# Low-rank products and head sums of a recurrence layer over all 128 columns of TensorE, in a four-layer model kernel

## The chip, the cores and the metric

The kernel runs on one core of one Trainium2 chip. The metric is the device time of one execution in microseconds (us). Before the change the median of 3 runs is 2441.49 us (2440.22 to 2445.58).

## The reference

The reference is a forward pass of four layers over 512 tokens of width 1024, in float32. Each layer has a mixer and a gated feed-forward net. The four mixers differ: a recurrence (RWKV-7), attention with a sliding window, a gated unit over chunks, and gated linear attention. The change touches the recurrence alone, `rwkv7_mix`, which computes, cut to what matters:

```python
xx = token_shift(x) - x
xr, xw, xk, xv, xa, xg = (x + xx * mu[c] for c in range(6))
r, k, v = jnp.einsum('cbsd,cde->cbse', jnp.stack([xr, xk, xv]), w_rkv).astype(f32)
w = -jax.nn.softplus(-(w0 + jnp.tanh(xw @ w1) @ w2).astype(f32)) - 0.5
a = jax.nn.sigmoid((a0 + (xa @ a1) @ a2).astype(f32))
g = jax.nn.sigmoid(xg @ g1) @ g2
kk = hs(k * k_k)
kk = kk * lax.rsqrt(jnp.maximum(jnp.sum(kk * kk, -1, keepdims=True), 1e-24))
```

There are 16 heads of 64 channels. `w1` and `a1` are 1024 x 64 and `g1` is 1024 x 128: these are the low-rank products. The sum of `kk * kk` over the channels of a head is the head sum. After this a state of 64 x 64 per head is carried over the 512 tokens; the kernel does that in chunks of 64 tokens, with a small triangular inverse for each.

## The kernel before

**Arithmetic.** Each float32 operand is split into a high and a low part of TensorE's faster float32 kind (`F32R`): ScalarE (ACT) copies the high part, VectorE (DVE) subtracts it to get the low one (`split`, line 617). A product is then three matmuls, high by high, high by low and low by high (`mm3`, line 621). `weights` (line 603) loads a weight of up to 1024 columns by a DMA on SyncE's queue (SP) and splits it. The recurrence stage has three raw buffers (`wraw`) and two buffers each for the high and low parts (`whi`, `wlo`), line 1066; 24 buffers of 512 columns (`slot`) hold split operands and, later, the work tiles of the recurrence (line 1067 and 1156).

**The recurrence stage**, `rwkv` (line 1050), in the order in which it is written:

1. `token_squares`, `rstd`: the norm of x. Constants: `sel`, 30 columns of zeros with two columns of ones for the two heads of a 128-row tile, and `selr`, its copy as F32R (lines 1075 to 1079).
2. For each of the eight 128-row tiles of x (line 1099): the normed tile `hn[k]`, its shifted difference `xx[k]`, the split of the weight rows `rw_w_k`, the mixed operand (`mixed`, line 1083: one DVE instruction for x + xx * mu, then a split), and 24 matmuls into the eight PSUM banks of the key product K.
3. Head sums (line 1113): for each of the eight tiles of K, ACT squares it, it is split, and two matmuls with 16 columns of `selr` as weights add into 16 rows of one bank.
4. The receptance product R in eight blocks `n` (line 1121), each with its own weight (`gemm`, line 627, 24 matmuls) over the same eight mixed operands. Between the blocks stand the tail of the head sums (line 1123: a copy of 16 rows, four transposes of 16 rows, the inverse root on DVE) and the low-rank products `lora` (line 1090): the one of `w1` behind block 0, of `a1` behind block 2, of `g1` behind block 4. Each loads and splits its weight and mixes its own eight operands, for 24 matmuls. The two 64-column products write 64 rows of a bank; their results are the two halves of `twa`.
5. The mixed operands of the value product V (line 1138).
6. `ahead(0)` (line 1158): for the first four heads `rwkv_prepare` (decays, from `twa` and the head sums), `rwkv_products`, `rwkv_inverse` (a long series of small DVE instructions) and `rwkv_direct`. Then the V product in two halves (line 1182), which is dense work for TensorE (PE).
7. Four times: `ahead(n + 1)`, and beside it `rwkv_chain` of n (line 1388), which walks the chunks in turn; at each, ACT copies PSUM results into `wu`, `tok` and `vu`, which the next matmuls need. `rwkv_out` (line 1459) finishes a group; its ACT instructions write `out`.
8. The output product, and then the feed-forward net and the other layers.

**Order.** The written order is not the order of issue. `Program` records all instructions and plans them (`run`, line 320): at each step it takes, over all engines, the instruction that could start first by its table of costs. On one engine the candidates are sorted by their turn, which is the number of the instruction as recorded plus the offset that the table `TURNS` (line 32) gives for its range of numbers; a candidate with a later turn is taken only where it could start over 200 ns sooner (`SLACK`). So a large positive offset makes a block filler, and a negative one puts it ahead. Buffers bound it too: an instruction isn't planned before a buffer of its pool is free. Where PE would idle, `keep_warm` and `ahead_of_cold` (lines 435 and 459) put in idle matmuls of `ident` (line 533).

By the recorded numbers the blocks of the change stand so: 0 to 408 are steps 1 to 3 with the mixing for R; 409 to 436 block 0 of R; 437 to 488 the low-rank product of `w1`; 489 to 516 block 1; 517 to 532 the tail of the head sums; 533 to 560 block 2; 561 to 612 `a1`; 613 to 640 block 3; 641 to 668 block 4; 669 to 720 `g1`; 721 to 804 blocks 5, 6 and 7; 805 to 852 the mixing for V; 853 to 910 `rwkv_prepare` of `ahead(0)`; 1236 to 1359 and 1360 to 1483 the halves of V. Later, 1499 to 1556, 2161 to 2218 and 2823 to 2880 are the three other `rwkv_prepare`, and 2090 to 2157, 2752 to 2819 hold the `rwkv_out` of groups 0 and 1's walks.

## Time and profile before

| | us |
|---|---|
| median of 3 runs | 2441.49 |
| the profiled execution | 2440.58 |
| its span, first to last instruction | 2438.9 |
| around the span | 1.7 |
| PE busy in the span | 2393.9 (98%) |
| DVE busy | 1952.3 (80%) |
| ACT busy | 1458.3 (60%) |
| granted TensorE clock, mean | 0.999 of full |

The recurrence stage takes about the first 436 us of the span. All instructions carry the line of the recording helper (L263), so groups are told apart by the names of their tiles: `ps<-slot,whi` is a matmul into a PSUM bank with the moving operand in a `slot` and the weights in `whi`. The form `128*64 128x512` is a matmul with 128 rows and 64 columns of weights, over 512 moving columns. `rw_w` is the tensor `rw_w1` or `rw_w2`, `rw_a` is `rw_a1` or `rw_a2` (the profile drops the number). Busy times of PE are modelled and overlap; where the pace of matmuls matters, the starts and their counts are used.

### The profile page before, as it was taken

What the parts mean: (1) busy time and instruction counts of PE and PEld (TensorE: products, weight loads), DVE (VectorE), ACT (ScalarE), POOL (GpSimd) and SP (SyncE); (2) the same over time, 40 slices, a digit from 0 to 9 for tenths busy, and PEclk for the clock granted to TensorE, in tenths of its full rate; (3) what the DMA queues carried; (4) which work ended last, traced back from release to release, by engine and by line L of the source; (5) the groups of instructions that cost most, each with busy time, mean ns of one, the idle gap of its engine ahead of it and who ended that gap; (6) DMA issues with size and microseconds to landing.
All of it is one profiled execution on the core that took longest, in us unless ns stands there. A gap on an engine that the chain in (4) does not pass through costs nothing.

```text
span 2438.9 us, 37676 instructions
## 1 busy us (share of the span) xinstructions
PE 2393.9 (98%) x14250; PEld 1974.5 (81%) x14250; DVE 1952.3 (80%) x3052; ACT 1458.3 (60%) x2389; POOL 337.7 (14%) x395
## 2 busy tenths in 40 slices
PE   9999999999999999999999999999999999999997
PEld 8677789988887759878777788898888888988885
DVE  8787875786889889768689879987868979886868
ACT  4656765665556697645466435755546756665554
POOL 0000000221212002112111300211111111221110
PEclk9999999999999999999999999999999999999999
DMA  5210013789986159889877836888997776998993
GB/s 174 77 61 10 6 39 109 151 219 233 207 223 168 36 142 201 208 202 218 199 181 190 219 101 148 182 218 212 221 227 192 176 178 141 207 211 218 223 220 87
DMA packets 128759, 404.55 MB, mean 166 GB/s; under 512 B 14512, under 2 KB 21680, under 8 KB 128576
## 3 DMA queue, kind: packets, MB, share of 16 engines
q0 software_dynamic: 51840, 176.18, 40.5%
q1 hardware_dynamic: 76736, 225.95, 27.4%
q8 instruction: 112, 1.84, 0.3%
q14 instruction: 71, 0.58, 0.1%
HBM read 397.62 MB, written 2.10 MB: 164 GB/s over the span
## 4 chain that ended last, share of the span: by engine, by line
PE 82%; DVE 7%; ACT 5%; issue 3%; DMA 2%; SPq 0%; POOL 0%; POOLq 0%; DVEq 0%; ACTq 0%
PE ps L263 82%; DVE slot L263 2%; DVE wlo L263 2%; ACT slot L263 1%; DMA wraw<-ffn_w_a 1%; DVE h L263 1%; ACT et L263 1%; ACT whi L263 1%; ACT out L263 1%; DVE left L263 1%; DMA wraw<-ffn_o_b 1%; ACT vu L263 0%; DVE et L263 0%; SPq L263 0%; DMA slot<-x 0%
## 5 line engine op out<-in xcount | busy, mean ns | idle before, releaser
L263 PE MATMUL ps<-whi,slot 128*128 128x512 f32 (+1 forms) x4944 | 1505.6, 385 | 11.8 <-ACT whi L263 6.4
L263 PEld LDWEIGHTS ps<-whi,slot 128*128 128x128 f32 x4944 | 916.6, 188 | 186.7 <-ACT whi L263 11.5
L263 ACT CAST whi<-wraw 128x1024 fp32r<-128x1024 f32 (+3 forms) x686 | 678.5, 997 | 573.5 <-PE ps L263 494.1
L263 DVE TENSOR_TENSOR wlo<-wraw,whi 128x1024 fp32r<-128x1024 f32 (+3 forms) x686 | 787.7, 1159 | 223.8 <-ACT whi L263 214.0
L263 PE MATMUL ps<-wlo,slot 128*128 128x512 f32 (+1 forms) x2472 | 929.1, 384 | 3.0 <-DVE wlo L263 2.8
L263 PEld LDWEIGHTS ps<-wlo,slot 128*128 128x128 f32 x2472 | 464.1, 188 | 88.3 <-DVE wlo L263 10.5
L263 PE MATMUL ps<-slot,whi 128*128 128x512 f32 (+3 forms) x976 | 280.6, 367 | 1.8 <-ACT slot L263 1.0
L263 PEld LDWEIGHTS ps<-slot,whi 128*128 128x128 f32 (+2 forms) x976 | 171.7, 184 | 40.0 <-DVE slot L263 3.0
L263 DVE TENSOR_TENSOR h<-h,ps 128x512 f32<-128x512 f32 x256 | 169.1, 682 | 29.9 <-PE ps L263 27.7
L263 DVE TENSOR_TENSOR slot<-ps,slot 128x512 f32<-128x512 f32 (+1 forms) x237 | 151.1, 650 | 44.2 <-PE ps L263 36.7
L263 POOL DMA_DIRECT2D wraw<-ffn_w_a x128 | 110.5, 873 | 514.1 <-DVE wlo L263 351.9
L263 PE MATMUL ps<-slot,wlo 128*128 128x512 f32 (+3 forms) x488 | 176.0, 365 | 0.1
L263 DVE TENSOR_TENSOR slot<-left,slot 128x512 fp32r<-128x512 f32 x254 | 160.1, 655 | 15.8 <-ACT slot L263 13.6
L263 ACT CAST slot<-left 128x512 fp32r<-128x512 f32 (+1 forms) x254 | 145.5, 600 | 33.1 <-DVE left L263 20.3
L263 ACT COPY slot<-ps 128x512 f32<-128x512 f32 (+3 forms) x168 | 89.1, 545 | 70.1 <-PE ps L263 69.0
L263 POOL DMA_DIRECT2D wraw<-ffn_w_b x64 | 55.0, 871 | 477.2 <-DMA wraw<-ffn_w_b 353.4
L263 PEld LDWEIGHTS ps<-slot,wlo 128*128 128x128 f32 (+2 forms) x488 | 89.6, 184 | 16.6 <-DVE wlo L263 1.7
L263 PE MATMUL ps<-ident,slot 128*128 128x128 f32 (+1 forms) x672 | 99.4, 267 | 3.1 <-DVE slot L263 2.9
L263 DVE TENSOR_TENSOR slot<-slot 128x512 fp32r<-128x512 f32 (+5 forms) x152 | 89.7, 613 | 7.0 <-ACT slot L263 5.0
L263 POOL DMA_DIRECT2D wraw<-ffn_o_a x64 | 55.6, 869 | 283.0 <-DVE wlo L263 180.4
L263 PEld LDWEIGHTS ps<-ident,slot 128*128 128x128 f32 (+1 forms) x672 | 67.4, 139 | 31.2 <-DVE slot L263 14.0
L263 DVE SCALAR_TENSOR_TENSOR slot<-slot,ncol 128x512 f32<-128x512 f32 (+1 forms) x96 | 66.9, 705 | 20.9 <-ACT slot L263 19.7
(285 smaller groups left out, 2190.6 us busy)
## 6 DMA issues: line engine op xcount, KB each, us to landing
wraw<-ffn_w_a SPq DMA_DIRECT2D x128, 512.0 KB, 6.0
wraw<-ffn_w_a POOLq DMA_DIRECT2D x128, 512.0 KB, 8.1
wraw<-ffn_o_a SPq DMA_DIRECT2D x64, 512.0 KB, 5.6
wraw<-ffn_o_a POOLq DMA_DIRECT2D x64, 512.0 KB, 6.6
wraw<-ffn_w_b SPq DMA_DIRECT2D x64, 384.0 KB, 4.7
wraw<-ffn_w_b POOLq DMA_DIRECT2D x64, 384.0 KB, 7.0
wraw<-ffn_o_b SPq DMA_DIRECT2D x16, 512.0 KB, 4.7
wraw<-ffn_o_b POOLq DMA_DIRECT2D x16, 512.0 KB, 7.9
```

The source lines that it names most:

```text
L263: op = self.add(eng.name, lambda: getattr(eng.target, what)(*map(real, args), **{k: real(a) for k, a in kw.items()}), *self.price(eng.name ...
```

## The change

- The head sums use 128 columns of weights and write all 128 rows of a bank. `selr` is now a `slot` of 142 columns: the 30 of `sel`, and zeros behind them that a second DVE copy writes. The tail copies 128 rows, makes four full transposes and reads the 16 wanted columns of each block.
- `w1` and `a1` go side by side into one raw tile by two DMAs (runs of 64 elements), are split together, and each of the two low-rank products uses all 128 columns, of which one half is used afterwards. Both are now written behind block 0 of R; `g1` is behind block 3 instead of 4.
- In the loop over the tiles of x, the mixed operand is written ahead of the split of the weight rows.
- With this the program has one instruction more ahead of number 410 and one fewer in all, so the ranges of `TURNS` shift, and the offsets of the recurrence stage are others. Those beyond number 4250 are the old ones, shifted by one.

In the numbering after the change, 410 to 437 is block 0 of R, 438 to 441 the loading of `w1` and `a1`, 442 to 490 the product of `w1`, 491 to 539 that of `a1`, 540 to 567 block 1, 568 to 583 the tail of the head sums, 584 to 611 block 2, 612 to 639 block 3, 640 to 691 `g1`, 692 to 719 block 4, 720 to 803 blocks 5 to 7; from 804 on each number is one less than before.

```diff
-    (0, 97, -207), (97, 193, -192), (193, 289, -140), (289, 409, -148), (437, 489, 1044), (489, 517, 10155), (517, 533, 2661), (533, 561, -359),
-    (561, 613, 1728), (641, 669, 1548), (669, 721, -310), (749, 777, 10951), (805, 853, 3322), (853, 911, 7335), (1190, 1236, -146),
-    (1236, 1360, -3686), (1360, 1484, 1692), (1499, 1557, 1650), (1557, 1577, -519), (1883, 1988, -731), (1988, 2090, -249), (2090, 2158, 1863),
-    (2161, 2219, 5511), (2239, 2259, -947), (2378, 2498, -3564), (2498, 2545, 2492), (2650, 2752, 2436), (2752, 2820, 5854), (2823, 2881, 3201),
-    (2881, 2901, -434), (2901, 2921, -32), (2921, 3040, 124), (3040, 3160, 418), (3207, 3312, -307), (3312, 3414, 300), (3414, 3483, 250),
-    (3483, 3588, -390), (3729, 3769, 843), (3886, 3999, 812), (4131, 4190, 149), (4350, 4449, 12), (4449, 4548, 141), (4548, 4647, -229),
...
+    (0, 98, -14563), (98, 194, -6331), (194, 290, -5109), (290, 410, -2326), (494, 540, 573), (568, 584, 3450), (612, 640, 6446), (640, 720, -1503),
+    (720, 748, 4169), (748, 776, -1620), (804, 852, 517), (852, 910, 9960), (910, 930, -70), (1189, 1235, -292), (1235, 1359, -995),
+    (1359, 1483, 955), (1498, 1556, 913), (1556, 1576, -521), (1835, 1882, 1053), (1882, 1987, -932), (1987, 2089, 433), (2089, 2157, 909),
+    (2160, 2218, 4894), (2377, 2497, -1662), (2497, 2544, 1319), (2544, 2649, -600), (2649, 2751, 2954), (2751, 2819, 9075), (2822, 2880, 7892),
+    (2920, 3039, 870), (3311, 3413, 750), (3413, 3482, 1012), (3627, 3728, 1237), (3728, 3768, 1131), (3772, 3885, -1758), (3998, 4112, 1412),
+    (4189, 4248, 51), (4349, 4448, 12), (4448, 4547, 141), (4547, 4646, -229), (4646, 4745, -100), (4745, 4844, -86), (4844, 4943, -93),
...
@@ -1075,8 +1074,9 @@
         nc.vector.memset(sel, 0.0)
         nc.vector.memset(sel[:64, 14:15], 1.0)
         nc.vector.memset(sel[64:, 15:16], 1.0)
-        selr = one("selr", F32R, 30)
-        nc.vector.tensor_copy(selr, sel)
+        selr = xp.tile([P, S], F32R, name="slot")[:, :14 + P]
+        nc.vector.tensor_copy(selr[:, 30:], sel[:, 0:1].to_broadcast([P, P - 16]))
+        nc.vector.tensor_copy(selr[:, :30], sel)
         near, rbc = self.rstd(ms)
         xx = []
 
@@ -1087,12 +1087,20 @@
             self.split(t, *x)
             return x
 
-        def lora(c, w, m, out, f):
-            hi, lo = self.weights(w, KT, m)
+        def pieces(w):
+            raw = self.wr.tile([P, 1024], F32, name="wraw").rearrange("p (k n) -> p k n", k=KT)
+            hi, lo = [l.tile([P, 1024], F32R, name=m).rearrange("p (k n) -> p k n", k=KT) for l, m in ((self.wh, "whi"), (self.wl, "wlo"))]
+            for j, t in enumerate(w):
+                t = t.rearrange("p (k n) -> p k n", k=KT)
+                nc.sync.dma_start(raw[:, :, j * 64:j * 64 + t.shape[-1]], t)
+            self.split(raw, hi, lo)
+            return hi, lo
+
+        def lora(c, w, r, out, f):
             ps = self.bank()
             for k in range(KT):
-                self.mm3(ps[:m], hi[:, k, :], lo[:, k, :], *mixed(c, k), k == 0, k == KT - 1)
-            nc.scalar.activation(out, ps[:m], f)
+                self.mm3(ps, w[0][:, k, :], w[1][:, k, :], *mixed(c, k), k == 0, k == KT - 1)
+            nc.scalar.activation(out, ps[r], f)
 
         rf, kf = [[keepers.tile([P, S], F32, name="rk") for _ in range(KT)] for _ in range(2)]
         ps = [self.bank() for _ in range(KT)]
@@ -1103,8 +1111,8 @@
             nc.vector.tensor_sub(b[:, 1:], hn[k][:, :S - 1], hn[k][:, 1:])
             nc.vector.tensor_scalar(b[:, 0:1], hn[k][:, 0:1], -1.0, None, op0=ALU.mult)
             xx.append(b)
+            x = mixed(2, k)
             hi, lo = self.weights(d['rw_w_k'][k * P:(k + 1) * P, :], 1, D)
-            x = mixed(2, k)
             for n in range(KT):
                 c = slice(n * P, (n + 1) * P)
                 self.mm3(ps[n], hi[:, 0, c], lo[:, 0, c], *x, k == 0, k == KT - 1)
@@ -1116,25 +1124,25 @@
             nc.scalar.activation(sq, kf[n], AF.Square, scale=v['rw_k_k'](n))
             self.split(sq, *part)
             for j in range(2):
-                nc.tensor.matmul(heads[:16], selr[:, 14 - 2 * n:30 - 2 * n], part[j], start=n + j == 0, stop=n + j == KT)
+                nc.tensor.matmul(heads, selr[:, 14 - 2 * n:14 - 2 * n + P], part[j], start=n + j == 0, stop=n + j == KT)
         x = [mixed(0, k) for k in range(KT)]
         for n in range(KT):
             self.gemm(d['rw_w_r'][n], x, lambda ps: nc.scalar.copy(rf[n], ps))
             if n == 1:
                 hs = tp.tile([P, S], F32, name="t")
-                nc.scalar.copy(hs[:16], heads[:16])
+                nc.scalar.copy(hs, heads)
                 ps = self.bank()
                 for b in range(NB):
-                    nc.tensor.transpose(ps[:, b * 16:(b + 1) * 16], hs[:16, b * P:(b + 1) * P], self.ident[:16, :16])
+                    nc.tensor.transpose(ps[:, b * P:(b + 1) * P], hs[:, b * P:(b + 1) * P], self.ident)
                 hc = self.sm.tile([P, NB * 16], F32, name="kkss")
-                nc.vector.tensor_scalar(hc, ps[:, :NB * 16], 1e-24, None, op0=ALU.max)
+                nc.vector.tensor_scalar(hc.rearrange("p (b h) -> p b h", b=NB), ps.rearrange("p (b h) -> p b h", b=NB)[:, :, :16], 1e-24, None, op0=ALU.max)
                 self.rsqrt(rs, hc)
             if n == 0:
-                lora(1, d['rw_w1'], 64, twa[:64], AF.Tanh)
-            if n == 2:
-                lora(4, d['rw_a1'], 64, twa[64:], AF.Identity)
-            if n == 4:
-                lora(5, d['rw_g1'], P, tg, AF.Sigmoid)
+                w = pieces((d['rw_w1'], d['rw_a1']))
+                lora(1, w, slice(0, 64), twa[:64], AF.Tanh)
+                lora(4, w, slice(64, P), twa[64:], AF.Identity)
+            if n == 3:
+                lora(5, pieces((d['rw_g1'],)), slice(0, P), tg, AF.Sigmoid)
         x = [mixed(3, k) for k in range(KT)]
         tall.close()
 
```

41 rows, old and new, of the table TURNS are left out of this document.

## The prediction

> **What bounds the kernel now.** I read the page first, then the busy time by stage.
>
> ```profile
> PE 2393.9 (98%) x14250; PEld 1974.5 (81%) x14250; DVE 1952.3 (80%) x3052; ACT 1458.3 (60%) x2389; POOL 337.7 (14%) x395
> ```
>
> ```profile
> core 0: us, PE busy (x) PEld busy (x) DVE busy (x) ACT busy (x) POOL busy (x), PEclk, DMA share, GB/s
> 19.18:68.06 48.88, 48.88 (x215) 40.29 (x216) 44.42 (x66) 25.29 (x38) 0.00 (x0) 1.00 0.34 106
> 68.06:136.72 68.66, 67.99 (x279) 44.99 (x277) 55.08 (x86) 40.74 (x65) 0.31 (x1) 1.00 0.24 72
> ...
> 190.88:380.00 189.12, 180.40 (x3159) 148.52 (x3160) 140.22 (x323) 133.60 (x288) 0.00 (x0) 1.00 0.09 28
> ...
> 436.80:2438.90 2002.10, 1970.99 (x9578) 1630.23 (x9576) 1624.17 (x2370) 1195.17 (x1888) 335.41 (x383) 1.00 0.79 187
> ```
>
> PE bounds the kernel: 98% busy at a granted clock of 1.00. 2002.10 of 2438.9 us lie behind the recurrence stage and are not edited, so the whole case lies in the first 436.8 us. There I see three parts. From 19.18 to 136.72 PE runs K, the head sums, R and the low-rank products; all of it must be done before the tiles of the recurrence can be placed (V's operands take the buffers that R's give back), so each matmul slot lost here shifts everything behind. From 136.72 on the V product gives PE dense work. From 190.88 to 380 small matmuls alternate with ACT and DVE, and no engine is full. How dense the first part is, the starts per 10 us tell:
>
> ```profile
> 30.00:40.00 10.00, 10.00 (x46) 8.29 (x45) 9.74 (x17) 3.25 (x4) 0.00 (x0) 1.00 0.35 100
> ...
> 70.00:80.00 10.00, 9.71 (x36) 4.55 (x34) 9.40 (x15) 9.32 (x16) 0.00 (x0) 1.00 0.17 54
> 80.00:90.00 10.00, 10.00 (x43) 7.65 (x43) 8.99 (x14) 7.47 (x11) 0.00 (x0) 1.00 0.30 88
> ...
> 100.00:110.00 10.00, 9.94 (x43) 7.22 (x44) 6.32 (x9) 5.13 (x9) 0.00 (x0) 1.00 0.15 31
> ```
>
> A dense stretch shows 46 matmuls. The head sums' stretch shows 36, so ten are missing, and the two quoted behind it, as the one between them, miss three each. The unit comes from the starts below (109.25 to 109.93, two `whi` and a `wlo`, three in 0.68 us): 0.227 us. So 2.3 us are lost from 70 to 80, where DVE (9.40) and ACT (9.32) are the bound, and 2.0 us from 80 to 110.
>
> **The change part by part.** *Wider weights.* The same 16 + 48 matmuls stay, over the same 512 moving columns.
>
> ```profile
> 68.06 0.40 PE L263 MATMUL ps<-slot,selr 128*16 128x512 f32 x1
> 68.30 0.39 PE L263 MATMUL ps<-slot,wlo 128*128 128x512 f32 x1
> 68.53 1.32 PE L263 MATMUL ps<-slot,selr 128*16 128x512 f32 x5
> 69.69 0.39 PE L263 MATMUL ps<-slot,whi 128*128 128x512 f32 x1
> ...
> 106.48 0.62 PE L263 MATMUL ps<-slot,whi 128*64 128x512 f32 x2
> ...
> 107.17 0.63 PE L263 MATMUL ps<-slot,whi 128*64 128x512 f32 x2
> ...
> 109.25 0.62 PE L263 MATMUL ps<-slot,whi 128*128 128x512 f32 x2
> ...
> 109.93 0.61 PE L263 MATMUL ps<-slot,whi 128*128 128x512 f32 x2
> ```
>
> Five with 16 columns take 1.16 us from start to start, 0.232 each; three with 64 (two `whi` and a `wlo`) take 0.69 (106.48 to 107.17), 0.230 each, against 0.227 with 128. So 16 x 0.005 + 48 x 0.003 = 0.2 us go; with the four transposes of 16 rows I take **-0.3**. A change of width shows no gap: the starts 68.06, 68.30 and 68.53 stand 0.24 and 0.23 apart. The Trainium skill, "TensorEngine Tiling (Array Packing)", section Key Properties, says that changing the tiling mode drains TensorE; these starts don't bear it out for columns, and what it would give stands with the rivals. Wider weights also load longer:
>
> ```profile
> L263 PEld LDWEIGHTS ps<-slot,whi 128*128 128x128 f32 x134 | 24.8, 188 | 7.8 <-DVE slot L263 1.3 <-ACT whi L263 1.0 <-ACT slot L263 0.9
> L263 PEld LDWEIGHTS ps<-slot,whi 128*64 128x64 f32 x32 | 4.2, 134 | 4.6 <-ACT rk L263 0.8 <-DVE slot L263 0.8 <-ACT slot L263 0.6
> L263 PEld LDWEIGHTS ps<-slot,selr 128*16 128x16 f32 x16 | 1.5, 93 | 3.8 <-DVE slot L263 2.2 <-ACT slot L263 1.0
> ```
>
> 48 x 54 + 16 x 95 ns = 4.1 us more of loading, hidden by the running matmul, since 188 ns is under the step of 227. Without that cover it is +4.1. The Trainium skill, "TensorE: Matmul & The Clock Gate", section LDWEIGHTS, speaks against the change here: the load's time scales with the columns. The rows agree in direction, but the pace of the 128-column rows shows it hidden.
>
> *One split instead of two.* ACT saves 2 x 0.62 - 1.05 = 0.19 us, DVE 2 x 0.69 - 1.22 = 0.15 us:
>
> ```profile
> L263 ACT CAST whi<-wraw 128x1024 fp32r<-128x1024 f32 x17 | 17.9, 1051 | 21.6 <-PE ps L263 19.3 <-DMA wraw<-rw_w_k 2.3
> L263 ACT CAST whi<-wraw 128x512 fp32r<-128x512 f32 x2 | 1.2, 619 | 2.3 <-PE ps L263 2.3
> ...
> L263 DVE TENSOR_TENSOR wlo<-wraw,whi 128x1024 fp32r<-128x1024 f32 x16 | 19.6, 1222 | 7.4 <-ACT whi L263 4.2 <-PE ps L263 2.8
> ...
> L263 DVE TENSOR_TENSOR wlo<-wraw,whi 128x512 fp32r<-128x512 f32 x2 | 1.4, 688 | 0.9 <-ACT whi L263 0.9
> ```
>
> It shortens the path only where PE waits for a split; of the larger saving I take **-0.2**. The two DMAs are the same in number, but in runs of 64 elements.
>
> ```profile
> 101.12 0.33 SPq L263 DMA_DIRECT2D wraw<-rw_a  x1
> ```
>
> ```profile
> wraw<-rw_a SPq DMA_DIRECT2D x1, 256.0 KB, 4.3
> ```
>
> ```profile
> 85.38 0.62 ACT L263 CAST whi<-wraw 128x512 fp32r<-128x512 f32 x1
> ...
> 114.03 0.62 ACT L263 CAST whi<-wraw 128x512 fp32r<-128x512 f32 x1 [2.26 <-PE ps L263]
> ```
>
> The DMA of `a1` was issued at 101.12 and landed 4.3 us later; its split began at 114.03, 12.9 us after issue and after a wait for PE, not for the DMA. That slack covers a landing three times as long, so I take nothing; on SP nothing urgent stands behind them. The second DVE copy of `selr` lies where DVE waits for x (8.1 us of idle, below): nothing.
>
> ```profile
> L263 DVE TENSOR_TENSOR slot<-t,slot 128x512 fp32r<-128x512 f32 x49 | 32.8, 688 | 8.3 <-PE ps L263 4.9 <-ACT slot L263 2.8
> L263 DVE SCALAR_TENSOR_TENSOR t<-xx,vec,h 128x512 f32<-128x512 f32 x42 | 30.4, 747 | 0.4
> ...
> L263 DVE BATCH_NORM_STATS2 xst<-slot 128x6 f32<-128x512 f32 x2 | 1.4, 694 | 8.1 <-DMA slot<-x 8.1
> ```
>
> The mixing moved ahead of the weight split lies at 16 to 62 us: the first matmul at 19.18 waits on the chain from the norm through `t`, not on a split, and later PE is dense (46 starts): nothing. The buffer that `selr` takes is given back with the head sums.
>
> *How long a pair of weight buffers is held.* There are two pairs of `whi` and `wlo`. While a low-rank product holds one, R's next split must wait for PE:
>
> ```profile
> ACT whi L263 <- PE ps L263: 15.0, 6, 4.9
> ```
>
> That row (84 to 126 us) is six splits that waited, and it is where the 2.0 us of 80 to 110 come from. `w1` held a pair from its split at 85.38 until matmuls of 128 columns alone run at 109.25, `a1` one from 114.03 until the row at 122.58:
>
> ```profile
> 122.58 0.62 PE L263 MATMUL ps<-slot,whi 128*128 128x512 f32 x2
> ```
>
> Now one pair is held for both. Run closely they need 48 x 0.227 = 10.9 us of PE, or 16 x (0.75 + 0.69) = 23 us of mixing on DVE by the means above, against some 32 us before. I take half of the loss back, **-1.0**; the ends are -2.0, and the rival below on the other side. The jam of 70 to 80 keeps its work on both engines: 0, with ends of 2.3 us either way.
>
> *The order behind.* The offsets of the whole stage are new, and no row prices an order. Block 1 of R, which `ahead(0)` needs, is no longer a filler (+10155 before, none now); blocks 3 and 5, needed later, are. The last `rwkv_prepare` (+3201 to +7892) and the `rwkv_out` behind the second walk (+5854 to +9075) are put off further, which lets ACT's copies for the walk go first. What they can give is seen in PE's longest group of waits from 190.88 to 380 and in the ACT work beside them:
>
> ```profile
> PE ps L263 <- ACT vu L263: 3.6, 9, 0.7
> ```
>
> ```profile
> L263 ACT ACTIVATE out<-v,bm,bonus 128x64 f32<-128x64 f32 x56 | 20.7, 432 | 0.1
> ```
>
> 20.7 us of `out` compete with the `vu` copies. The bound is PE's idle time there, 189.12 - 180.40 = 8.7 us, all regained or as much added. I take the waits for `vu`, **-3.6**. What is late next is DVE (140 of 189 us busy).
>
> Sum: -0.3 - 0.2 - 1.0 - 3.6 = -5.1. The profiled execution took 2440.58 (1.7 around its span, 0.9 under the median of 2441.49), so **2435.5**.
>
> **The rivals.** *Nothing to measure:* the new order only moves idle time about, and the three small terms remain: 2440.58 - 1.5 = 2439. For it: 8.7 us of idle is all there is behind, and each block put off must still run. Against: it is a new order throughout, and that it nets to nothing would be chance. If the longer loads show, 2440.58 + 4.1 = 2444.7, which is also too little to tell.
>
> *Slower, by the shared pair:* `a1`'s product has the turn 491 + 573 = 1064, behind blocks 1 (540), 2 (584) and 7 (776) and behind V's first half (1235 - 995 = 240), `w1` is at 442. If `a1` waits for its turn, the pair is held over those splits, and R and V run with one pair. Each boundary then costs PE up to an ACT split, 1.05 us plus 0.05, where no low-rank matmul is at hand to fill it. Eight boundaries (three of R, four tiles of V's half, and block 5) are 8.8 us, less the 2.0 already lost: +6.8, so 2447.4. It decides from the second boundary on (2 x 1.1 = 2.2). For it: the 15.0 us of waits above. Against: V's tiles need buffers that R's operands hold, so V can hardly run ahead.
>
> *The drain:* if each of the 31 changes of width (16 or 64 to 128 and back, counted in the starts from 68.06 to 122.58) cost PE what the slowest did, all go.
>
> ```profile
> 91.74 1.40 PE L263 MATMUL ps<-slot,whi 128*64 128x512 f32 x4
> 92.98 0.39 PE L263 MATMUL ps<-slot,wlo 128*64 128x512 f32 x1
> ```
>
> Four starts in 1.24 us are 0.33 over the pace: 31 x 0.33 = 10.2, so 2430. Against it stand the starts at 68 us, and that a split ended at 92.1. It is the skill's rule named above.
>
> **How the numbers follow.** The forecast, faster by more than 0.2%, has 0.36, and the drain 0.04: together 0.40. Nothing to measure has 0.34 (0.02 of it for the loads). Slower has 0.26: 0.20 for the shared pair, 0.06 for an order that adds idle time. About 0.2%, 4.9 us, is what a measurement of this kernel can tell from no change. The likeliest case's own range is 2428 to 2436.6. The range of all reaches down by the ends of hold, jam and order, 2440.58 - 2.0 - 2.3 - 8.7 = 2427.6, and up to the shared pair's 2447.4 with room for part of the order's loss: **2427 to 2449**.
>
> **What would show it.** Right: no matmul with 16 or 64 columns at 512 moving ones; 128-wide ones at 0.227 from start to start; V beginning near 135 instead of 136.72; a shorter wait of PE on `vu`; the feed-forward net beginning near 431 instead of 436.8, and from there on the same length as before. Wrong: one `whi` tile with low-rank matmuls spread over more than 32 us; fewer than 43 starts in the stretches from 80 to 110; an inverse that begins later than before; or a difference that arises behind 436.8 us, where I expect none.

## The result, and the profile after

The changed kernel is slower: a median of 2448.9 us against 2442.2 us for the kernel before, in 16 executions of each. The ratio of their times is 1.0024 with a 95% interval of 1.0017 to 1.0032, so +5.9 us (4.2 to 7.8); the medians themselves lie 6.7 us apart. That is inside the range and on the wrong side of the forecast. Below, every difference is a ratio to the kernel before on the same chip, times 2442.2 us; the intervals are 2 to 3 us to either side.

The changed kernel's page, its line of busy times (its profiled execution took 2446.15 us, its span is 2444.5; its helper stands at L262, its idle matmuls at L532):

```profile
PE 2402.4 (98%) x14252; PEld 1984.5 (81%) x14252; DVE 1951.6 (80%) x3052; ACT 1458.1 (60%) x2388; POOL 337.6 (14%) x395
```

PE was busy 8.5 us longer with 14252 matmuls instead of 14250, and idle for 42.1 us instead of 45.0. So the loss is not idle time; it hides in a "busy" PE. The stretches of the changed kernel show where, by the number behind the x:

```profile
68.06:136.72 68.66, 68.66 (x288) 50.82 (x287) 57.27 (x95) 43.19 (x68) 1.64 (x6) 1.00 0.26 83
190.88:380.00 189.12, 181.18 (x3051) 147.60 (x3047) 138.61 (x322) 124.62 (x266) 0.00 (x0) 0.99 0.03 8
441.80:2444.50 2002.70, 1972.71 (x9583) 1631.34 (x9581) 1623.18 (x2371) 1195.38 (x1888) 335.26 (x383) 1.00 0.79 187
```

From 68.06 to 136.72 us PE starts 288 matmuls instead of 279: the first part gained. From 190.88 to 380 us it is busier than before (181.18 against 180.40 us) and starts 108 matmuls fewer (3051 against 3159). The feed-forward net shows the sum; its first matmuls, in the kernel before and in the changed kernel:

```profile
435.63 0.95 PE L263 MATMUL ps<-whi,rk 128*128 128x512 f32 x3
```

```profile
441.80 1.17 PE L262 MATMUL ps<-whi,rk 128*128 128x512 f32 x4
```

It begins 6.17 us later and ends 2002.7 us after that (2003.3 before: 2438.9 - 435.63). All of the loss lies ahead of it, and by its starts the first part has no share in it. The first part of the changed kernel, in stretches of 10 us:

```profile
70.00:80.00 10.00, 10.00 (x41) 6.68 (x40) 8.93 (x14) 9.17 (x15) 0.00 (x0) 1.00 0.40 107
80.00:90.00 10.00, 10.00 (x44) 7.43 (x44) 9.97 (x15) 7.95 (x11) 0.00 (x0) 1.00 0.22 79
100.00:110.00 10.00, 10.00 (x45) 7.92 (x44) 9.75 (x18) 4.83 (x8) 0.31 (x1) 1.00 0.18 53
```

41, 44 and 45 starts where there were 36, 43 and 43. And PE's longest groups of waits from 190.88 to 380 us, in the changed kernel (total us, times, longest):

```profile
PE ps L262 <- DVE bonus L262: 1.5, 1, 1.5
PE ps L532 <- DVE st L262: 1.3, 1, 1.3
PE ps L262 <- ACT wu L262: 1.3, 3, 0.5
PE ps L262 <- ACT vu L262: 0.8, 3, 0.4
```

The wait that I wanted to shorten did get shorter, from 3.6 to 0.8 us, and no time came of it.

### The profile page after: what moved, and what is told of

It reads as the page before. It is cut to its first block, busy times and chain, and to the rows that moved or that the text cites. A ratio compares the mean times of both kernels' runs of the same rounds, so it can differ in the third digit from the quotient of the medians.

```text
span 2444.5 us, 37687 instructions
## 1 busy us (share of the span) xinstructions
PE 2402.4 (98%) x14252; PEld 1984.5 (81%) x14252; DVE 1951.6 (80%) x3052; ACT 1458.1 (60%) x2388; POOL 337.6 (14%) x395
## 4 chain that ended last, share of the span: by engine, by line
PE 84%; DVE 7%; ACT 5%; issue 3%; DMA 1%; POOL 0%; DVEq 0%; ACTq 0%; POOLq 0%
PE ps L262 83%; DVE slot L262 2%; DVE wlo L262 2%; ACT slot L262 2%; DMA wraw<-ffn_w_a 1%; DVE h L262 1%; ACT whi L262 1%; PE ps L532 1%; ACT et L262 1%; DVE left L262 1%; ACT out L262 1%; ACT vu L262 0%; DVE et L262 0%; DVE rs_t L262 0%; DVE mt L262 0%
## 5 line engine op out<-in xcount | busy, mean ns | idle before, releaser
L262 PE MATMUL ps<-whi,slot 128*128 128x512 f32 (+1 forms) x4944 | 1506.8, 385 | 10.6 <-ACT whi L262 5.9
L262 PEld LDWEIGHTS ps<-whi,slot 128*128 128x128 f32 x4944 | 916.7, 188 | 186.2 <-ACT whi L262 11.9
L262 ACT CAST whi<-wraw 128x1024 fp32r<-128x1024 f32 (+2 forms) x685 | 678.1, 998 | 565.3 <-PE ps L262 480.2
L262 DVE TENSOR_TENSOR wlo<-wraw,whi 128x1024 fp32r<-128x1024 f32 (+1 forms) x685 | 785.9, 1159 | 218.0 <-ACT whi L262 209.3
L262 PE MATMUL ps<-wlo,slot 128*128 128x512 f32 (+1 forms) x2472 | 929.6, 384 | 3.7 <-DVE wlo L262 3.3
L262 PEld LDWEIGHTS ps<-wlo,slot 128*128 128x128 f32 x2472 | 464.1, 188 | 89.7 <-DVE wlo L262 12.2
L262 PE MATMUL ps<-slot,whi 128*128 128x512 f32 (+2 forms) x976 | 281.5, 367 | 1.6 <-ACT slot L262 1.0
L262 PEld LDWEIGHTS ps<-slot,whi 128*128 128x128 f32 (+1 forms) x976 | 173.3, 185 | 37.0 <-ACT whi L262 3.2
L262 DVE TENSOR_TENSOR h<-h,ps 128x512 f32<-128x512 f32 x256 | 169.1, 682 | 30.0 <-PE ps L262 27.9
L262 DVE TENSOR_TENSOR slot<-ps,slot 128x512 f32<-128x512 f32 (+1 forms) x237 | 151.0, 649 | 44.4 <-PE ps L262 36.7
L262 POOL DMA_DIRECT2D wraw<-ffn_w_a x128 | 110.4, 874 | 513.2 <-DVE wlo L262 355.3
L262 PE MATMUL ps<-slot,wlo 128*128 128x512 f32 (+2 forms) x488 | 176.6, 365 | 0.0
L262 DVE TENSOR_TENSOR slot<-left,slot 128x512 fp32r<-128x512 f32 x254 | 160.0, 655 | 15.8 <-ACT slot L262 13.6
L262 ACT CAST slot<-left 128x512 fp32r<-128x512 f32 (+1 forms) x254 | 145.6, 600 | 32.7 <-DVE left L262 20.3
L262 ACT COPY slot<-ps 128x512 f32<-128x512 f32 (+3 forms) x168 | 89.0, 545 | 67.5 <-PE ps L262 66.5
L262 POOL DMA_DIRECT2D wraw<-ffn_w_b x64 | 55.0, 870 | 491.0 <-DMA wraw<-ffn_w_b 357.4
L262 PEld LDWEIGHTS ps<-slot,wlo 128*128 128x128 f32 (+1 forms) x488 | 90.5, 186 | 14.8 <-DVE wlo L262 0.8
L262 PE MATMUL ps<-ident,slot 128*128 128x128 f32 (+1 forms) x672 | 99.3, 267 | 3.1 <-DVE slot L262 2.8
L262 POOL DMA_DIRECT2D wraw<-ffn_o_a x64 | 55.2, 863 | 284.1 <-DVE wlo L262 186.2
L262 DVE TENSOR_TENSOR slot<-slot 128x512 fp32r<-128x512 f32 (+5 forms) x152 | 89.7, 613 | 5.4 <-ACT slot L262 3.3
L262 PEld LDWEIGHTS ps<-ident,slot 128*128 128x128 f32 (+1 forms) x672 | 67.5, 139 | 30.5 <-DVE slot L262 14.0
L262 DVE SCALAR_TENSOR_TENSOR slot<-slot,ncol 128x512 f32<-128x512 f32 (+1 forms) x96 | 66.9, 704 | 20.9 <-ACT slot L262 19.7
```

Of the source, the lines that this page charges most:

```text
L262: op = self.add(eng.name, lambda: getattr(eng.target, what)(*map(real, args), **{k: real(a) for k, a in kw.items()}), *self.price(eng.name ...
```

## The experiments

Most of these kernels are one of the two programs with another order of issue. The planner is replaced by a list of the recorded numbers; the operations, tiles and sizes stay. `old` and `new` are the two kernels' lists in one numbering, `upto(a, b, K)` is the first K steps of a, then all that is left in the order of b:

```diff
     with tc.manual_schedule():
-        prog.run()
+        issue(prog, ORDER)
```

### Is it the order or the forms?

```diff
+ORDER = upto(new, old, 950)    # changed kernel: after_then_before_160
+ORDER = upto(old, new, 950)    # kernel before: before_then_after_162
```

> The changed kernel's operations, issued in the changed kernel's order for the first 950 steps (up to about 160 us) and from there in the order of the kernel before. Theory A (the loss is the order of the later part: the put-off preparation and output of the recurrence's last sub-steps): the 6 us go, and what PE had gained by 160 us (1.1 us by the summed gaps between matmuls; 2.7 us at 136 us) stays: 2439.5 to 2441.5, that is 0.7 to 2.7 us under the kernel before. Theory B (the wider forms, the shared pair of weight tiles or the start of the stage cost it, and the later part only inherits a delay): about 2449, as the changed kernel. Theory C (both halves): 2443 to 2447.

> The reverse: the operations of the kernel before, none of the change in them, in their own order for the first 950 steps (about 162 us), then in the order that the changed kernel has. Theory A: the loss appears without the change: 2448 to 2451 (6 us over the kernel before, plus up to 2 us since the gain of the first part is missing). Theory B: about 2442, as the kernel before. Theory C: 2444 to 2447.

Measured: 0.9995 (0.9986 to 1.0004), -1.2 us, and 1.0020 (1.0010 to 1.0030), +4.9 us. The loss appears without the change and is gone with the change in the old order. The feed-forward net begins accordingly, in the first run and in the second:

```profile
435.15 0.93 PE L262 MATMUL ps<-whi,rk 128*128 128x512 f32 x3
```

```profile
442.78 1.17 PE L263 MATMUL ps<-whi,rk 128*128 128x512 f32 x4
```

PE's row for `vu` in the first is that of the kernel before, in the second that of the changed kernel:

```profile
PE ps L262 <- ACT vu L262: 3.6, 9, 0.7
```

```profile
PE ps L263 <- ACT vu L263: 0.8, 3, 0.4
```

So the short wait goes with the slow order, and the long one with the fast.

### Where along the stage?

```diff
+ORDER = upto(new, old, 2240)                   # changed kernel: after_then_before_272
+ORDER = upto(new, old, 2950)                   # changed kernel: after_then_before_334
+ORDER = upto(new, old, 3450)                   # changed kernel: after_then_before_375
+ORDER = upto(old, new, 3450)                   # kernel before: before_then_after_372
+ORDER = upto(upto(old, new, 950), old, 2950)   # kernel before: new_order_160_to_335
+ORDER = upto(upto(old, new, 950), old, 2350)   # kernel before: new_order_160_to_284
+ORDER = upto(upto(old, new, 2391), old, 2950)  # kernel before: new_order_284_to_335
```

> The same with the seam at step 2240 (about 272 us, where walk 1's first state update has just been issued: 271.75 us in the changed kernel, 273.6 before). Theory A, with all of the loss behind the seam: 2440 to 2442.5. If part of it arose between 160 and 272 us (the summed gaps of PE show 1.0 us given back there): up to 1.5 us more than with the seam at 160 us. Theory B: about 2449.

> The same with the seam at step 2950 (about 334 us, at walk 2's first state update, which comes at 333.95 us in the changed kernel and at 327.38 us before). Theory A with two losses, one in front of walk 2 (6.6 us late there, of which some 3 to 4 us stand in PE's summed gaps at 350 us) and one behind it (the loads for the output product at 377.9 us instead of 355.6 us; another 2.5 us of gaps up to 400 us): 2445 to 2447. If the first alone makes the loss: about 2449; if the second alone does: about 2442.5. Theory B: about 2449.

> The changed kernel's operations in its own order up to step 3450 (about 375 us, just ahead of walk 3's first state update) and in the order of the kernel before from there: walk 3, the output product and their loads. All against the kernel before; the changed kernel stands at +5.9 us, the seam at 334 us gave +2.0, the one at 160 us -1.2. If walk 3 with the output product is where the order loses most (PE's summed gaps grow by 2.5 us between 370 and 390 us and by 0.5 to 1.4 us up to 430): +2 to +3.5. If the loss lies between 334 and 375 us, in walk 2's steps behind ahead(3)'s products: +5 to +6, as without the seam. If it is spread over all stretches: about +3.5 to +4.5.

> The reverse: the kernel before, nothing of the change in it, in its own order up to step 3450 (about 372 us) and then in the changed kernel's order. If walk 3 with the output product in the new order costs by itself: +2 to +4, with walk 3's state updates some 11 us apart instead of 3 to 6, and the feed-forward net's first matmuls later by as much. If walk 3 in that order is only late because its inverse is (walk 2 ends at 364.0 us instead of 356.25): 0 to +1.

> The kernel before, in the changed kernel's order only between steps 950 and 2950 (some 160 to 335 us: walks 0 and 1, the second and third inverse, up to walk 2's first state update), its own order ahead of it and behind. If the loss adds up over the stretches: +2 to +3.5 here, and with the run above (the new order from 372 us) about the +4.9 that the new order from 162 us on gave. If it stands in this stretch (the put-off preparation of ahead(3) delays walk 2 and with it all that follows): +4 to +6. If what is late here is made up behind, as the seams at 272 and 334 us suggest (+1.5 and +2.0 with the changed front, which alone gave -1.2): +2.5 to +3.5 as well, but with walk 2's first st near 335 us and the gaps of PE ahead of it.

> The kernel before, in the changed kernel's order only from step 950 (some 160 us) up to walk 1's fourth state update (284.8 us), its own order ahead and behind. The new order from 160 to 335 us gave +6.8 us (ratio 1.0028). If what costs is the preparation of ahead(3) and the output behind walk 1, which are put off further: their operations stand behind this seam, so 0 to +1.5 here. If the loss is spread evenly over the stretch: +2.5 to +4. If it stands in walk 0 and the second inverse: +5 to +7.

> The rest of that stretch: the kernel before, in the changed kernel's order only from walk 1's fourth state update to walk 2's first. If the put-off pieces cost: +4 to +7, with a wait of PE for the state update near 298 us (1.5 us in the changed kernel, behind the third inverse's chain on DVE) and walk 2's first st at 332 to 335 us. If the loss is spread: +2.5 to +4. If it stands ahead of 284 us: 0 to +1.5.

Measured, in this order: 1.0006 (+1.5 us), 1.0008 (+2.0), 1.0040 (+9.8), 1.0007 (+1.7), 1.0028 (+6.8), 1.0025 (+6.1) and 1.0013 (+3.2). The seam at 375 us missed all three of its expectations, and the stretch from 160 to 335 us came out just above its highest. The two halves, 6.1 and 3.2, add up to more than their whole, 6.8, though not beyond the intervals. The seam at 375 us costs more than the whole new order (+9.8 against +5.9), so a seam can cost by itself, and these runs can't share the loss out: they show that the stretch from 160 to 335 us in the new order is enough to make it, and that the last walk in the new order is not (+1.7, -0.5 to +3.9). With the seam at 375 us the old order wants the output product at once, while its weights are loaded only then. ACT splits them ahead of its copies for the walk, and PE waits 5.55 us for `vu`; from within that wait on the granted clock is low, 0.54 from 383 to 394 us:

```profile
386.67 0.70 PE L262 MATMUL ps<-vu,tok 128*64 128x64 f32 x8 [5.55 <-ACT vu L262]
```

```profile
383.00:394.00 11.00, 7.33 (x53) 6.76 (x54) 4.22 (x11) 4.69 (x12) 0.00 (x0) 0.54 0.44 160
```

On SP's queue, in the changed kernel itself:

```profile
377.50 0.33 SPq L262 DMA_DIRECT2D g<-rw_g  x1
377.93 2.43 SPq L262 DMA_DIRECT2D et<-rw_w_o  x5
```

The new order had put the product behind the late loads. Each order seems to fit only itself.

### Three suspects in the traces

The changed kernel with single pieces moved. At walk 2's start PE stands before ahead(3)'s products, and the loads above come 22 us later than before, behind a load that waits for a buffer.

```diff
+move([3215..3222], ahead_of=3274); move([3229], ahead_of=3278)          # walk2_first
+move([3230..3233], ahead_of=3328); move([3234, 3235], ahead_of=2888)    # walk2_first
+move([3768..3772, 3799, 3826, 3857, 3884], ahead_of=2821)               # loads_first
```

> The changed kernel with one place of its order altered: walk 2's first step (the eight products of the inverse with its right-hand side, the copy of vu, the four products with tok, the two state updates st) is issued ahead of the product matmuls and mask multiplications of ahead(3), behind which it waits from 325.4 to 332.0 us in the changed kernel. All times against the kernel before, to which the changed kernel stands at +5.9 us. If the block at walk 2's start is a loss of its own (2.6 us in PE's summed gaps between 310 and 350 us): +2 to +4. If it is covered, because walk 3 waits for ahead(3)'s inverse anyway (its second half is done at 370.5 us in the changed kernel, 369.5 before) and the next step of walk 2 still stands behind the same products: +5 to +7, with the first st near 327 us and walk 3's first st still at 376 to 378 us. If what is put behind it is ahead(3)'s inverse, which sets walk 3: above +7.

> The changed kernel with another place altered: on SP's queue the four loads of the residual input and the first five loads of the output weights stand ahead of the g2 load for sub-step 3, which waits for one of two lp buffers until 377.5 us and holds them until 377.9 to 383 us (354.6 to 371 us before). If the late loads are the loss behind 334 us (seams at 334 us and at the end differ by 0.0016, 3.9 us, and PE's summed gaps by 1.9 us): +2 to +4 against the kernel before, with the first of the output weights at or before 356 us, the output product's matmuls between walk 3's steps, and walk 3's last st at 400 to 410 us instead of 423.9. If those matmuls could not have run earlier anyway (their place in PE's order lies behind walk 3's first steps): +5 to +6, the same trace but for SP.

> Both alterations together. If each mends a loss of its own: the sum of the two gains, +0 to +2.5 against the kernel before. If one hides behind the other: no better than the better of the two. If neither matters: +5 to +7.

Measured: 1.0022 (+5.4 us), 1.0020 (+4.9) and 1.0027 (+6.6). None differs from the changed kernel's +5.9. Walk 2's first state update, on DVE in walk2_first (333.95 us in the changed kernel), and the loads in loads_first:

```profile
324.52 0.59 DVE L262 TENSOR_TENSOR st<-ps,pend 64x128 f32<-64x128 f32 x2 [0.83 <-PE ps L262]
336.15 0.42 DVE L262 TENSOR_TENSOR st<-ps,pend 128x256 f32<-128x256 f32 x1 [0.41 <-PE ps L262]
```

```profile
367.70 3.13 SPq L262 DMA_DIRECT2D et<-rw_w_o  x5
```

The first update came 9.4 us sooner and the second 1.6 us: it stood behind the same products. The loads came 10 us sooner, not the 22 us by which they are late, and PE's place for the product stayed. So two delays that are plain to see in the trace were undone in part, by 9.4 and 10 us, and that gained nothing that these runs can tell.

### The two blocks of my step

```diff
+ORDER = old with 2823..2880 where new has them     # kernel before: preparation_put_off
+ORDER = new with 2751..2818 where old has them     # changed kernel: output_as_before
```

> The kernel before with one block of operations alone where the changed kernel has it: the preparation of ahead(3) (offset +3201 before, +7892 changed; its part on DVE stands some 50 to 80 steps later, its part on ACT up to 40 steps earlier or later); all others keep their order. My prediction had this as a gain (-3.6 us together with the output behind walk 1, by ACT's copies for the walk going first). If it is instead the piece that costs: +2 to +5. If the order of the small pieces among one another costs, and no block by itself: -1 to +1.5.

> The changed kernel with the other block alone put back to where the kernel before has it: the output behind walk 1 (offset +9075 in the changed kernel, +5854 before), whose products with g2 hold an lp buffer until 377.5 us in the changed kernel. If this block's delay costs: +2 to +4 against the kernel before instead of +5.9, with the g2 load for sub-step 3 and the loads behind it some 20 us earlier. If not: +5 to +7.

Measured: 1.0044 (1.0032 to 1.0057), +10.7 us, and 1.0068 (1.0054 to 1.0081), +16.6 us. Both missed all that was expected of them. In the first, two copies into `pend` had to go behind a state update as well, since their buffers come free there. From 290 to 330 us, in it and in the kernel before:

```profile
290.00:330.00 40.00, 33.85 (x601) 28.31 (x602) 26.87 (x64) 18.77 (x37) 0.00 (x0) 0.87 0.02 5
```

```profile
290.00:330.00 40.00, 38.67 (x771) 33.22 (x771) 36.38 (x87) 27.19 (x53) 0.00 (x0) 1.00 0.02 6
```

PE starts 170 matmuls fewer, at a granted clock of 0.87, which alone is some 5 of the 40 us. Putting the preparation off, with these two copies, is a loss by itself, where my step saw a gain. But taking the output back to its old place, which was to mend half of the loss, cost 10.7 us more than the changed kernel's own order; there the granted clock is 0.86 from 370 to 395 us. Neither block is "the" piece.

### Forms and the shared pair

```diff
-                nc.tensor.matmul(heads[:16], selr[:, 14 - 2 * n:30 - 2 * n], part[j], ...
+                nc.tensor.matmul(heads, selr[:, 14 - 2 * n:14 - 2 * n + P], part[j], ...   # kernel before: head_sums_wide (cut)
```

> One form alone: the 16 head-sum matmuls over 128 columns instead of 16, with the copy, the four transposes and the maximum that belong to it; all else and the whole order as before. My term for it was about -0.1 us (16 matmuls at 0.232 instead of 0.227 us and the four transposes). The rival of a drain at each change of width had 0.33 us each: 31 changes stand in the stretch, most of them at the head sums, so -5 to -8 us here. What the changed kernel's trace shows of it: 36 changes of form between 62 and 136 us took 1.67 us over the pace of their matmuls before, 46 ns each, and 2 remain; so -0.5 to -1.5 us, seen in PE's summed gaps from 62 to 100 us but too little to tell in the time.

Measured: 1.0007 (0.9998 to 1.0016), +1.7 us. From 62 to 136 us, in it, in the kernel before and in the changed kernel:

```profile
62.00:136.00 74.00, 73.44 (x302) 50.61 (x301) 58.07 (x89) 45.80 (x73) 0.31 (x1) 1.00 0.21 67
```

```profile
62.00:136.00 74.00, 73.33 (x302) 49.35 (x301) 58.11 (x90) 46.26 (x74) 0.31 (x1) 1.00 0.22 69
```

```profile
62.00:136.00 74.00, 74.00 (x310) 54.54 (x309) 60.05 (x99) 48.46 (x77) 1.64 (x6) 1.00 0.25 81
```

302 starts with 16 columns, 302 with 128: the width gives nothing that shows, and the 5 to 8 us that a drain would have given back aren't there. The changed kernel's eight more are 8 x 0.227 = 1.8 us.

```diff
+ORDER = old, each new operation where its counterpart stands   # changed kernel, head sums as before
+move([split of the last R block], behind=[last product of a1])  # pair_in_before_order
```

> The forms without the new order: the three low-rank products over all 128 columns, with two weights sharing one pair of weight tiles, and the first operand mixed ahead of the weight split, but the head sums as before (16 columns), and every operation at the place that its counterpart has in the order of the kernel before, in the early part too. One pair of operations cannot stay: a third pair of weight tiles would be needed, so the split of the last R block's weights waits for the last low-rank product. My sum for the wider weights and the saved split was -0.5 us, and the price that I set on a pair that is held too long was +6.8 us. If the pair held long costs nothing at the end (the operands for the V products run beside it): -2 to +1. If the rival has its price: +3 to +8, with PE's gaps in 100 to 136 us and V's first matmul later than 136.7 us.

Measured: 1.0025 (1.0014 to 1.0035), +6.1 us. In 100 to 136 us of it PE has 33.18 us of 36 and 137 starts (35.68 and 149 in the kernel before), and no split of weights begins between these two:

```profile
105.80 1.05 ACT L262 CAST whi<-wraw 128x1024 fp32r<-128x1024 f32 x1 [4.87 <-PE ps L262]
120.41 1.04 ACT L262 CAST whi<-wraw 128x1024 fp32r<-128x1024 f32 x1
```

That is the rival of the shared pair: V's first matmul comes at 139.34 us instead of 136.72. But the 12 missing starts are 2.7 us, not 6.1. The profiled execution, at 2443.44 us and a granted clock of 0.999, is the quickest of eleven; their median is 2449.17, and the slowest seven have a clock of 0.995 to 0.996. So the trace shows less than half of the price, and the rest goes with a lower clock in executions of which there is no trace. The changed kernel escapes the jam by its order: there the pair is split at 91.44 us, and `a1`'s result is taken at 120.01, with other splits beside it.

### The arrangement itself

```diff
+ORDER = exchange(upto(new, old, 950))   # changed kernel: rearranged_from_old_order
+ORDER = exchange(new)                   # changed kernel: rearranged_from_new_order
```

> The changed kernel's operations in its order up to step 900, then in the order of the run after_then_before_160 (0.9995 of the kernel before), rearranged up to step 4450 (some 150 to 450 us) by many small exchanges of neighbouring pieces on PE, ACT and DVE, each kept only where a sum over the durations, dependencies and buffers of all operations came out shorter. PE changes the form of its matmuls less often in it. Nothing is left out, added or resized. If what the changed kernel lost is how its operations stand among one another, a better arrangement must gain as surely as the new one lost: -3 to -10 us against the kernel before, with fewer changes of form between 160 and 450 us than 187 (before: 189, changed kernel: 216, at some 0.12 us each) and PE's summed gaps there shorter by as much. If an arrangement that is right by such a sum isn't so on the chip (the changed kernel's was made by one too, and is 5.9 us over): -1 to +6.

> The same rearranging, begun from the changed kernel's own order (+5.9 us against the kernel before, 216 changes of form between 160 and 450 us). If the new order's loss can be undone by small exchanges: -8 to 0 against the kernel before. If it is in the larger layout, which such exchanges do not reach (the put-off preparation of ahead(3), the output behind walk 1, the loads behind it): +2 to +5, with walk 2's first st still near 330 us. If the sum misleads: +5 or more.

Measured: 0.9952 (0.9940 to 0.9965), -11.7 us, and 0.9974 (0.9963 to 0.9985), -6.3 us. Both beat both kernels, with the changed kernel's operations and nothing but the order altered. The first one's stretch, and its first matmuls of the feed-forward net:

```profile
190.88:380.00 189.12, 179.58 (x3225) 151.60 (x3222) 144.45 (x346) 142.88 (x311) 0.00 (x0) 1.00 0.08 27
```

```profile
423.37 0.94 PE L262 MATMUL ps<-whi,rk 128*128 128x512 f32 x3
```

3225 starts, in less busy time than the changed kernel's 3051. The net begins 12.3 us sooner than in the kernel before, but this execution, at 2433.99 us the slowest of its five, then takes 2008.9 us instead of 2003.3, with 3.4 us at half clock at 1049 us. And its waits:

```profile
PE ps L262 <- ACT vu L262: 3.4, 7, 1.1
PE ps L262 <- DVE mt L262: 2.4, 4, 1.0
```

The fastest order waits for `vu` nearly as long as the kernel before.

What differs is shown by the time between the starts of neighbouring matmuls, from 160 to 450 us. Over the median step of two matmuls of the same form (rows x columns of the weights, and the moving shape), I sum the excess at each change of rows or columns, and that of all single gaps over 0.25 us (a change with such a gap counts as a gap alone):

```
                             changes of form, us over pace   gaps > 0.25 us   all over pace
kernel before                     189         22.5               12.4             65.6
changed kernel                    216         25.1               11.9             72.1
after_then_before_160             187         22.8               13.9             67.0
before_then_after_162             215         25.5               14.1             72.7
rearranged_from_old_order         138         16.0               13.7             55.4
rearranged_from_new_order         139         15.7               14.2             58.7
```

A change costs 0.113 to 0.122 us throughout. The new order has 27 more of them, +2.6 of the 6.5 us; the fastest has 51 fewer, -6.5 of -10.2. The long gaps, which a view of waits names, hardly move in these six (-0.5 and +1.3). The rest, +4.4 and -5.0, is small excess that no change of form and no long gap explains. Three runs that the table leaves out, the slowest of all, lose in another way: by the same sums `output_as_before`, `preparation_put_off` and `after_then_before_375` have at most 3 us more than the kernel before at changes of form, but some 6 to 10 us more in gaps over 0.25 us. One piece of the changed kernel shows what changes cost, eight products of `tok` and `vu` taken in turns with transposes (three of the four pairs are shown):

```profile
374.18 0.27 PE L262 MATMUL ps<-ident,out 128*128 128x128 f32 x1
374.59 0.33 PE L262 MATMUL ps<-vu,tok 128*64 128x64 f32 x2
374.85 0.33 PE L262 MATMUL ps<-ident,out 128*128 128x128 f32 x1
375.11 0.33 PE L262 MATMUL ps<-vu,tok 128*64 128x64 f32 x2
375.37 0.33 PE L262 MATMUL ps<-ident,out 128*128 128x128 f32 x1
375.63 0.33 PE L262 MATMUL ps<-vu,tok 128*64 128x64 f32 x2
375.88 0.48 PE L262 MATMUL ps<-tg,g 128*128 128x256 f32 x1
```

In the fastest order:

```profile
368.07 0.45 PE L262 MATMUL ps<-vu,tok 128*64 128x64 f32 x8
368.36 0.63 PE L262 MATMUL ps<-vu,pr 128*64 128x64 f32 x8
```

Eight in a row take 0.29 us to the next start. The five short pieces from 374.59 to 375.88 take 0.26 each. No idle time stands at any of these rows.

## Why the prediction was wrong

**Wider weights (-0.3):** nothing that can be measured, and no drain that shows where the moving side has 512 columns: 302 starts either way, as above. The longer loads stayed hidden, too.

**One split, and the pair held less long (-0.2 and -1.0):** right as far as the starts tell; no run has these terms by themselves in the new order. ACT's waits for PE ahead of a split, 84 to 126 us, in the changed kernel:

```profile
ACT whi L262 <- PE ps L262: 9.5, 5, 4.0
```

15.0 us before. The pair was held from 91.44 to about 120 us, 28.6 us instead of some 32. Together with the jam of 70 to 80 us, where I took 0 and five starts came back, the first part gained 1.8 us by its starts. The feared shared pair is real in the old order (+6.1, of which the trace shows 2.7). That its 2447.4 us lies near the measured time is luck: V began earlier here, not later.

**The order behind (-3.6):** this step failed, in sign. It said that the last `rwkv_prepare` and the `rwkv_out` behind the second walk, "put off further", let "ACT's copies for the walk go first", and took the waits for `vu`. The waits fell by 2.8 us as said, and the order cost 4.9 us by itself (before_then_after_162). Two errors are in it. It sized an order by one row of waits, although all the rows of PE's waits from 190.88 to 380 us are only some 8 us (8.4 before, 7.3 in the changed kernel, 8.8 in the fastest), with no relation to these times; in the runs of the two blocks they are 13.4 and 11.8 us. And its bound, 8.7 us of idle time, did not bound: PE's busy time held more than that, by 22.5 us at changes of form alone, and an order is free to raise or lower it. My rival "an order that adds idle time" had the right place with a chance of 0.06 and the wrong mark, for PE's busy time in the stretch rose from 180.40 to 181.18 us.

**The drain:** I weighed the Trainium skill's "TensorEngine Tiling (Array Packing)", section Key Properties (a changed tiling mode drains TensorE), against the starts at 68 us and set it aside. There, beside matmuls of 512 moving columns, the head sums made wide bear that out. From 160 us on, where 64x64 alternates with 128x128 over 64 or 128 moving columns, a change stands at 0.12 us on average, which is the direction of the rule; I had looked for it in the one place where it doesn't show.

**Signs:** V began at 129.27 us, ahead of the last R block, not near 135; the last inverse began later (ACT's first copy for it at 333.1 instead of 326.7 us), the sign that I had named for wrong; behind the stage nothing changed, as said.

**Slips in its working:** the trace has 33 changes of width from 68.06 to 122.58 us where it counts 31; `a1`'s offset begins at number 494, so its turn is 1067, not 1064; and block 5's turn (720 + 4169) lies behind that, so by the turns the shared pair had seven boundaries, not eight. None of them decides anything.

**Still open:** which exchanges make the new order slow. Changes of form are 2.6 of 6.5 us over the pace; the larger part is small excess within a form, 1.7 us of it in one stretch of half clock (below). No run altered the number of changes and nothing else, so that each causes its 0.12 us is read from the traces and not isolated.

## What to carry to other kernels

When a change comes with a new order of issue, test the order by itself: run the old operations in the new order and the new ones in the old. In a stage of many small matmuls, don't size an order by the rows of waits; count the matmuls started per stretch and how often neighbours differ in form. A delay that is plain in the trace may cost nothing, so undo it before believing in it. And look at the granted clock of all executions of a run, for its trace shows only one of them.

## What I had not expected of the hardware

Beside the 0.12 us per change of form, which no busy or idle time shows: short stretches of half clock in an otherwise full kernel. In the changed kernel's profiled execution:

```profile
243.00:247.00 4.00, 3.82 (x20) 3.83 (x20) 3.97 (x9) 1.62 (x3) 0.00 (x0) 0.57 0.01 4
```

At 0.57 over 4 us, 1.7 us go. More exactly the clock is 0.50 for 3.41 us from 243.20. In the 3.41 us just ahead PE was busy for half of the time:

```profile
239.79:243.20 3.41, 1.74 (x13) 0.86 (x9) 3.17 (x10) 3.40 (x6) 0.00 (x0) 1.00 0.01 2
```

Apart from 9 to 11 us at the end of each execution, the kernel before had no such stretch in its profile. The other traces have 22 of them, at other places, 3.41, 6.83 or 10.24 us long (the longest from 383 us in `after_then_before_375`, from within the wait of 5.55 us on), and ahead of 21 of them PE was busy less than 0.6 of 3.41 us. Stretches as thin pass without one, too, so this is no rule yet. The Trainium skill, "TensorE: Matmul & The Clock Gate", section "What's actually happening", has a free-running window of 3413 ns, which fits the length.

Runs of one kernel lie some 6 us apart (2439.8 to 2445.6 before), and a part of that goes with the clock: in the changed kernel the quickest executions have 0.998, the slowest 0.996. It does not make the difference measured here: the mean granted clock of the changed kernel's 16 executions is 0.998, as is that of the kernel before in each experiment. But some orders do run at a lower one: 0.995 on the mean in `after_then_before_375`, 0.996 in `output_as_before`, `preparation_put_off` and `new_order_160_to_284`, 0.997 in `pair_in_before_order`. A thousandth of the clock over 2440 us is 2.4 us, as an estimate, so half or so of what three of these lose (+9.8, +6.1 and +6.1) goes this way.
